# fp16 tiles transposed as 32-bit words on TensorE, for all tiles, in a matmul with rotary embedding

## The chip, the cores and the metric

One core of one Trainium2 chip runs the whole program. The metric is device time in microseconds; the kernel before took 157.14 us, the median of two runs (156.81 and 157.47).

## The reference

`x` is 16 x 512 x 768, `weight` 768 x 768, `cos` and `sin` 512 x 64, all fp32; there are 12 heads of 64. A matrix product is followed by a rotation of each head's two halves with factors that depend on the position in the sequence:

```python
y = np.matmul(x, weight).reshape(batch, seq, n_heads, head_dim)
y1, y2 = y[..., :32], y[..., 32:]
out1 = y1 * cos1 - y2 * sin1        # cos1, sin1: the first halves of cos and sin
out2 = y2 * cos2 + y1 * sin2        # cos2, sin2: the second halves
out = np.concatenate([out1, out2], axis=-1).reshape(batch, seq, hidden)
```

## The kernel before

The 8192 rows of `x` are cut into 64 tiles of 128 rows, and four tiles make a group (16 groups, numbered 0 to 15). The contraction over 768 is cut into six chunks of 128, named (t, e) with t of 3 and e of 2. Chunk (t, e) takes the columns of `x` whose index m x 6 + t x 2 + e runs over m = 0 to 127, and the rows of `weight` to match. TensorE (PE) needs each chunk of a tile with its columns on the partitions, so a tile has to be transposed before it is multiplied.

A tile goes through these steps:

- SyncE (SP) issues a DMA of the tile into one of ten buffers `xs` (`load`, L192). `pump` issues loads ahead as far as `xs` buffers are free; a buffer counts as free once its cast has been issued.
- ScalarE (ACT) casts it to fp16 into one of five buffers `xc` (`cast`, through the helper `copy`, so its line is L172). The output is contiguous in the order t, m, e; the input is read in pairs 24 bytes apart.
- PE transposes the six chunks, 128 x 128 fp16 each, into one PSUM bank `pt`, of which there are two (`turn`, L238). The data is the weight that PE loads (LDWEIGHTS), the identity `ident` is streamed.
- ACT copies the six results, 768 fp16 contiguous, into one of eight buffers `xt` (L172 as well). For tiles 0 and 1 VectorE (DVE) does this copy.
- PE multiplies: six chunks into each of two pieces of the tile's 768 output columns (512 and 256), 12 matmuls, summed in PSUM `py`, six banks (`mm_piece`, L302).
- DVE multiplies 1024 output columns at a time by cos and by sin (`rope`, L320), GpSimd (POOL) adds the two products into `ov` (L331), and `store` (L352) sends half a group at a time to memory, issued on ACT's queue. The last group goes in smaller pieces.

Twenty of the 64 tiles are not transposed on PE. `BLOCKS` names ten pairs: tiles 2 and 3 of each group from 5 to 14. A pair is loaded in four quarters (`load_quarter`, L207) laid out so that 32 x 32 blocks are what remains to be turned, and DVE turns it in one instruction, two fp16 as one 32-bit word (`turn_pair`, L263). In odd groups SP loads the pair as fp32 and ACT casts both tiles at once (`cast_pair`, L172); in even groups POOL's DMA converts to fp16 on the way and no cast is needed.

The order on every engine is written out by hand; the class `Flow` only adds semaphore waits where a buffer is read or reused. In the main loop over tiles i = 4 to 63 each iteration issues the 12 matmuls of tile i, then DVE's pair transposes (`bturns`), then PE's transposes up to tile i + `T_AHEAD` (3; tile i + 2 in the first two iterations), then the casts up to tile i + `C_AHEAD` (7), then POOL's pair loads, then the stores of the group before (after the first and third tile of a group). The prologue handles tiles 0 to 3 together with six weight chunks, which SP loads (`load_w`, L214) and DVE casts; L356 to L358 clear `cold` and build `ident`, and L413 runs twelve matmuls on zeros at the start.

Of the kernel before, what the change touches and what calls it, by code (L numbers as in the profile page):

```python
# [10 lines left out]
FP32 = mybir.dt.float32  # L11
FP16 = mybir.dt.float16
# [91 lines left out]
def kernel(  # L104
# [19 lines left out]
    R = 32  # L124
    NQ = P // R
# [9 lines left out]
    BLOCKS = {}  # L135
    for g in range(5, 15):
        BLOCKS[g, 1] = "pool" if g % 2 == 0 and g >= 4 else "sp"

    def sbuf(name, shape, dt):
        return nc.alloc_sbuf_tensor(name, shape, dt).ap()  # L140

    NX, NB, NBH, NC, NCP, NXT, NXP, NTQ, NOV = 10, 3, 3, 5, 2, 8, 4, 3, 4

    ident = sbuf("ident", [P, P], FP16)
# [6 lines left out]
    xb_b = [sbuf(f"xb{i}", [P, 2 * H], FP32) for i in range(NB)]  # L151
    xh_b = [sbuf(f"xh{i}", [P, 2 * H], FP16) for i in range(NBH)]
    xc_b = [sbuf(f"xc{i}", [P, H], FP16) for i in range(NC)]
    xd_b = [sbuf(f"xd{i}", [P, 2 * H], FP16) for i in range(NCP)]
    xt_b = [sbuf(f"xt{i}", [P, NT, 2, P], FP16) for i in range(NXT)]
    xp_b = [sbuf(f"xp{i}", [P, 2 * H], FP16) for i in range(NXP)]
# [22 lines left out]
    def pair_of(i):  # L179
        return i // QB, (i % QB) // 2  # L180

    def is_block(i):
        return pair_of(i) in BLOCKS

# [10 lines left out]

    def load_quarter(gh, q):
        g, h = gh
        b, r = where(g * QB + 2 * h)
        e = BLOCKS[gh]
        src = x[b : b + 2].rearrange("b (j a r) (q k) -> r q a (b j) k", r=SB, a=R, q=NQ)  # L200
        if q == 0:
            xs[gh] = ring("xh", NBH) if e == "pool" else ring("xb", NB)
        k = xs[gh]
        name = f"xh{k}" if e == "pool" else f"xb{k}"
        buf = xh_b[k] if e == "pool" else xb_b[k]
        dst = buf.rearrange("p (j k) -> p j k", j=2 * NQ)
        do(e, lambda eng: eng.dma_start(out=dst[ts(q, R)], in_=src[r, q]),  # L207
           writes=[f"{name}q{q}"], dma=name)
# [14 lines left out]
    def cast(i, e):  # L223
        k = xs[i]
        c = ring("xc", NC)
        xc[i] = c
        do(e, copy(e, xc_b[c].rearrange("p (t m e) -> p t m e", t=NT, e=2),
                   xs_b[k].rearrange("p (m t e) -> p t m e", t=NT, e=2)),
           reads=[f"xs{k}"], writes=[f"xc{c}"])

    def turn(i, e):
        c = xc[i]
        k = ring("pt", 2)
        z = ring("xt", NXT)
        src = xc_b[c].rearrange("p (t m e) -> p t e m", t=NT, e=2)
        pt = pt_b[k].bitcast(FP16)[:, 0:H].rearrange("p (t e m) -> p t e m", t=NT, e=2)
        for t, h in CHUNKS:
            do("pe", lambda eng: eng.transpose(pt[:, t, h, :], src[:, t, h, :], ident),  # L238
               reads=[f"xc{c}", "ident"], writes=[f"pt{k}"], tick=(t, h) == CHUNKS[-1])
        do(e, copy(e, xt_b[z], pt), reads=[f"pt{k}"], writes=[f"xt{z}"])  # L240
        xT[i] = (lambda t, h: xt_b[z][:, t, h, :], f"xt{z}")

    def cast_pair(gh, e="act"):
        k = xs[gh]
        c = ring("xd", NCP)
        xc[gh] = c
        do(e, copy(e, xd_b[c].rearrange("p (t j e) -> p t j e", t=NT, e=2),
                   xb_b[k].rearrange("p (j t e) -> p t j e", t=NT, e=2)),
           reads=[f"xb{k}q{q}" for q in range(NQ)], writes=[f"xd{c}"])

    def turn_pair(gh):
        g, h = gh
        z = ring("xp", NXP)
        dst = xp_b[z].bitcast(FP32)
        if BLOCKS[gh] == "pool":
            k = xs[gh]
            src = xh_b[k].bitcast(FP32).rearrange("p (j t) -> p t j", t=NT)
            rd = [f"xh{k}q{q}" for q in range(NQ)]
        else:
            c = xc[gh]  # L260
            src, rd = xd_b[c].bitcast(FP32), [f"xd{c}"]
        v = xp_b[z].rearrange("p (t m e) -> p t e m", t=NT, e=2)
        do("dve", lambda eng: eng.transpose(out=dst, in_=src), reads=rd, writes=[f"xp{z}"])  # L263
        for s in (0, 1):
            xT[g * QB + 2 * h + s] = (
                lambda t, e, s=s: v[:, t, e, ts(s, P)], f"xp{z}")


# [28 lines left out]
    def mm_piece(i, piece, c, start, stop, tick):  # L297
        g, s = divmod(i, QB)
        a, z, ps, bank = piece
        get, key = xT[i]  # L300
        t, h = c
        do("pe", lambda eng: eng.matmul(  # L302
            ps, get(t, h), w_sb[:, t, h, a - s * H : z - s * H], start=start, stop=stop),
            reads=[key, f"w{t}{h}"], writes=[bank], tick=tick)
# [56 lines left out]

    order = [0, 1, "w0", 2, "w1", "w2", 3, "w3", "w4", "w5"]
# [11 lines left out]
    fetch, quarters = [], []  # L374
    soon = [p for p in sorted(BLOCKS) if BLOCKS[p] == "sp"]
    for i in range(QB, NTILE):
        if soon and i >= max(2, soon[0][0] - 1) * QB:
            quarters += [(soon[0], q) for q in (0, 2, 1, 3)]
            soon.pop(0)
        if not is_block(i):  # L380
            fetch.append(i)
            if quarters:
                fetch.append(quarters.pop(0))
        elif quarters and quarters[0][0] == pair_of(i):
            fetch.append(quarters.pop(0))
    fetched = [0]
    xs_used, xb_used = [0], [0]
    xs_sent, xb_sent = [4], [0]

    def pump():  # L390

        while fetched[0] < len(fetch):
            j = fetch[fetched[0]]
            if isinstance(j, int):
                if xs_sent[0] - xs_used[0] >= NX:
                    return
                load(j)
                xs_sent[0] += 1
            else:
                if j[1] == 0:  # L400
                    if xb_sent[0] - xb_used[0] >= NB:
                        return
                    xb_sent[0] += 1
                load_quarter(*j)
            fetched[0] += 1
# [55 lines left out]
    assert not quarters  # L461
    pump()

    state = {"cast": 4, "turn": 4, "bturn": 0, "pool": 0}
    pairs = sorted(BLOCKS)
    pool_pairs = [p for p in pairs if BLOCKS[p] == "pool"]

    def casts(upto):
        while state["cast"] < min(upto, NTILE):
            i = state["cast"]  # L470
            state["cast"] += 1
            if not is_block(i):
                castx(i, "act")
            elif i % 2 == 0 and BLOCKS[pair_of(i)] == "sp":
                cast_pair(pair_of(i))
                xb_used[0] += 1
            pump()

    def turns(upto):
        while state["turn"] < min(upto, NTILE):  # L480
            i = state["turn"]
            state["turn"] += 1
            if not is_block(i):
                turn(i, "act")

    def bturns(upto):
        while state["bturn"] < len(pairs):
            gh = pairs[state["bturn"]]
            if gh[0] * QB + 2 * gh[1] >= upto:
                return  # L490
            turn_pair(gh)
            state["bturn"] += 1

    def pool_loads(upto):
        while state["pool"] < len(pool_pairs):
            gh = pool_pairs[state["pool"]]
            if gh[0] * QB + 2 * gh[1] >= upto:
                return
            for q in (0, 2, 1, 3):
                load_quarter(gh, q)  # L500
            state["pool"] += 1

    C_AHEAD, T_AHEAD, B_AHEAD, P_AHEAD = 7, 3, 6, 20
# [18 lines left out]
    for i in range(QB, NTILE):  # L522
        g, s = divmod(i, QB)
        us = units(g)
        done_to = (s + 1) * H
        for p in pieces(g, s):
            a, z, _, bank = p
            for c in CHUNKS:
                mm_piece(i, p, c, c == CHUNKS[0], c == CHUNKS[-1],
                         tick=c == CHUNKS[-1])  # L530
            for u in us:
                if u[1] == z:
                    rope(g, u)
        bturns(i + (B_AHEAD if i >= SETTLED else 3))
        turns(i + 1 + (T_AHEAD if i > QB + 1 else 2))
        casts(i + 1 + (C_AHEAD if i >= SETTLED else 3 if i == QB else 4))
        pool_loads(i + P_AHEAD)
        if s == 0 and g > 0:
            store(g - 1, 0, 2 * H, "act")
        if s == 2 and g > 0:  # L540
            store(g - 1, 2 * H, 4 * H, "act")
        if g == LAST:
            if s == 2:
                store(g, 0, H, "sp")
            if s == 3:
                store(g, H, 2 * H, "act")
# [42 lines left out]
```

## Time and profile before

| | |
|---|---|
| runs | 156.81 and 157.47 us, median 157.14 |
| profiled execution | 156.38 us, span of its instructions 154.6 us, mean granted TensorE clock 0.991 |
| PE, matmul records | 145.2 us busy, 94% of the span, 1056 instructions |
| DVE | 125.8 us, 81%, 82 instructions |
| POOL | 123.4 us, 80%, 79 instructions |
| ACT | 77.4 us, 50%, 92 instructions |
| chain that ended last | PE 84%, DVE 4%, DMA 4%, ACT 2% |
| DMA | 51.16 MB, mean 331 GB/s; 27548 packets, 7184 of them under 512 B |

A span runs from the first to the last instruction; the execution's time has 1.8 us more. Busy time is summed over a whole run whose stages differ, so a share near 100% names a suspect only. Matmuls are pipelined: a matmul's record spans from its start to its modelled end and overlaps the next one, so PE's rhythm is read from starts or from the chain, not from mean durations. L172 is the line of a helper that makes every cast and copy, and the names of the tiles tell these apart. The idle time beside a group is the wait of the engine ahead of it, with what ended it.

### The profile page before, as it was taken

The numbers are of one execution on the slowest core, as the hardware profiler recorded it, in microseconds if no ns is written. First come the engines' busy times: TensorE is split into PE (matmuls) and PEld (weight loads), VectorE is DVE, ScalarE is ACT, GpSimd is POOL, SyncE is SP. The second block draws the span as 40 slices with busy tenths as digits, with TensorE's granted clock in tenths as the row PEclk, the third lists the DMA queues.
The fourth block names the chain that finished last, engine by engine and source line by source line (L and its number), as shares of the span: only waits on it lengthen the run. The fifth ranks groups of instructions, "written<-read, shape, count | busy, mean of one in ns | idle before, by whom it ended". The sixth has DMA issues, their size and how long they took to land.

```text
span 154.6 us, 2609 instructions
## 1 busy us (share of the span) xinstructions
PE 145.2 (94%) x1056; PEld 91.9 (59%) x1056; DVE 125.8 (81%) x82; ACT 77.4 (50%) x92; POOL 123.4 (80%) x79
## 2 busy tenths in 40 slices
PE   6799999999999999999999999999999999999930
PEld 2345566666666666566666666665666666666720
DVE  0436997688777979998999899898999899997990
ACT  3462959699658615744282707452483418243000
POOL 1000599799888999799989999899988886999940
PEclk9999999999999999999999999999999999999996
DMA  4999999999999999999999999999999963443983
GB/s 138 387 408 397 403 399 401 368 342 362 372 344 302 395 350 336 358 381 363 351 332 385 391 347 318 365 405 368 368 368 360 382 251 139 155 179 150 374 336 106
DMA packets 27548, 51.16 MB, mean 331 GB/s; under 512 B 7184, under 2 KB 13072, under 8 KB 27536
## 3 DMA queue, kind: packets, MB, share of 16 engines
q1 hardware_dynamic: 13504, 24.78, 45.7%
q10 hardware_dynamic: 8592, 24.25, 39.9%
q0 software_dynamic: 5440, 1.97, 10.3%
q8 instruction: 8, 0.13, 0.3%
q14 instruction: 4, 0.03, 0.1%
HBM read 27.79 MB, written 25.17 MB: 343 GB/s over the span
## 4 chain that ended last, share of the span: by engine, by line
PE 84%; DVE 4%; DMA 4%; ACT 2%; SPq 1%; issue 1%; DVEq 0%
PE py L302 76%; PE pt L238 9%; DMA w_raw<-in_weight_dram 4%; DVE xs L320 1%; ACT xc L172 1%; DVE tq L320 1%; DVE ov L331 1%; SPq L192 1%; DVE w_raw L320 1%; SPq L214 1%; ACT xt L172 1%; DVE w_sb L172 0%; DVEq L55 0%; SPq L584 0%; SPq L114 0%
## 5 line engine op out<-in xcount | busy, mean ns | idle before, releaser
L302 PE MATMUL py<-w_sb,xt 128*128 128x256 f16 (+1 forms) x528 | 89.9, 323 | 1.4 <-DVE w_sb L172 1.1
L331 POOL TENSOR_TENSOR ov<-tq 128x1024 f32<-128x1024 f32 (+2 forms) x33 | 68.9, 2105 | 21.6 <-DVE tq L320 21.4
L320 DVE TENSOR_TENSOR tq<-py,csn 128x2048 f32<-128x2048 f32 (+2 forms) x33 | 66.4, 2024 | 9.3 <-PE py L302 8.9
L302 PEld LDWEIGHTS py<-w_sb,xt 128*128 128x128 f16 x528 | 50.3, 98 | 32.6 <-DVE w_sb L172 2.8
L172 ACT COPY xt<-pt 128x768 f16<-128x768 f16 x42 | 33.5, 800 | 56.1 <-PE pt L238 56.1
L320 DVE TENSOR_TENSOR w_raw<-py,csn 128x2048 f32<-128x2048 f32 (+1 forms) x20 | 41.4, 2068 | 5.8 <-PE py L302 5.7
L331 POOL TENSOR_TENSOR ov<-w_raw 128x1024 f32<-128x1024 f32 (+1 forms) x20 | 42.8, 2149 | 2.6 <-DVE w_raw L320 2.6
L172 ACT CAST xc<-xs 128x768 f16<-128x768 f32 x44 | 39.2, 905 | 8.6 <-DMA xs<-in_x_dram 8.4
L302 PE MATMUL py<-w_sb,xp 128*128 128x512 f16 (+1 forms) x240 | 42.3, 326 | 0.0
L302 PEld LDWEIGHTS py<-w_sb,xp 128*128 128x128 f16 x240 | 22.6, 98 | 12.9
L238 PE MATMUL pt<-ident,xc 128*128 128x128 f16 x264 | 21.9, 219 | 0.2 <-ACT xc L172 0.2
L238 PEld LDWEIGHTS pt<-ident,xc 128*128 128x128 f16 x264 | 18.0, 98 | 6.8 <-ACT xc L172 2.0
L207 POOL DMA_DIRECT2D xh<-in_x_dram x20 | 11.7, 590 | 0.0
L172 ACT CAST xd<-xb 128x1536 f16<-128x1536 f32 x5 | 8.0, 1603 | 0.0
L263 DVE STREAM_TRANSPOSE xp<-xh 128x768 f32<-128x768 f32 x5 | 6.2, 1246 | 0.0
L172 DVE CAST w_sb<-w_raw 128x768 f16<-128x768 f32 x6 | 3.4, 559 | 3.5 <-DMA w_raw<-in_weight_dram 3.5
L413 PE MATMUL py<-cold 128*128 128x512 f16 x12 | 4.6, 552 | 1.4 <-DVE cold L356 1.4
L172 DVE COPY xt<-pt 128x768 f16<-128x768 f16 x2 | 1.1, 558 | 4.8 <-PE pt L238 4.8
L263 DVE STREAM_TRANSPOSE xp<-xd 128x768 f32<-128x768 f32 x5 | 4.8, 968 | 0.0
L413 PEld LDWEIGHTS py<-cold 128*128 128x128 f16 x12 | 1.4, 131 | 3.4 <-issue 1.9
L172 ACT ACT_TABLE_LOAD x1 | 1.3, 1283 | 0.9 <-SPq L114 0.9
L302 PE MATMUL pt<-w_sb,xt 128*128 128x256 f16 x12 | 1.5, 272 | 0.0
(13 smaller groups left out, 6.8 us busy)
## 6 DMA issues: line engine op xcount, KB each, us to landing
out_dram<-ov ACTq DMA_DIRECT2D x30, 768.0 KB, 8.3
xs<-in_x_dram SPq DMA_DIRECT2D x44, 384.0 KB, 16.2
xb<-in_x_dram SPq DMA_DIRECT2D x20, 192.0 KB, 16.5
w_raw<-in_weight_dram SPq DMA_DIRECT2D x6, 384.0 KB, 6.7
xh<-in_x_dram POOLq DMA_DIRECT2D x20, 96.0 KB, 12.3
out_dram<-ov SPq DMA_DIRECT2D x1, 384.0 KB, 2.8
out_dram<-ov ACTq DMA_DIRECT2D x1, 384.0 KB, 2.5
out_dram<-ov SPq DMA_DIRECT2D x1, 256.0 KB, 2.0
```

The lines of the kernel that those rows point to most:

```text
L172: eng.copy(out=o, in_=i_) if e == "act" else eng.tensor_copy(out=o, in_=i_)
L192: do(e, lambda eng: eng.dma_start(out=xs_b[k], in_=x[b].rearrange("(p r) h -> r p h", r=SB)[r]), writes=[f"xs{k}"], dma=f"xs{k}")
L207: do(e, lambda eng: eng.dma_start(out=dst[ts(q, R)], in_=src[r, q]), writes=[f"{name}q{q}"], dma=name)
L214: do(e, lambda eng: eng.dma_start(out=w_raw[:, t, h], in_=wv[t, h]), writes=[f"wr{t}{h}"], dma=f"w{t}{h}")
L238: do("pe", lambda eng: eng.transpose(pt[:, t, h, :], src[:, t, h, :], ident), reads=[f"xc{c}", "ident"], writes=[f"pt{k}"], tick=(t, h) == ...
L263: do("dve", lambda eng: eng.transpose(out=dst, in_=src), reads=rd, writes=[f"xp{z}"])
L302: do("pe", lambda eng: eng.matmul(ps, get(t, h), w_sb[:, t, h, a - s * H : z - s * H], start=start, stop=stop), reads=[key, f"w{t}{h}"], w ...
L320: do("dve", lambda eng: eng.tensor_tensor(out=tq.rearrange("p j (h d) -> p j h d", d=D), in0=ps.rearrange("p (h d) -> p h d", d=D) .unsque ...
L331: do(adder, lambda eng: eng.tensor_tensor(out=ov_b[o][:, ds(c0, w)].rearrange("p (h t d) -> p h t d", t=2, d=HD), in0=tq[:, 0].rearrange(" ...
L413: do("pe", lambda eng: eng.matmul(py[:, ts(b, 512)], cold[:, 0:P], cold, start=True, stop=warmed[0] < WARM - 6), reads=["cold"], writes=[f ...
```

## The change

All 64 tiles now take the same way, and the pairs with their loads, casts, buffers and DVE transposes are gone. `xc` has room for a 32-bit word per value. The cast writes each fp16 into the lower half of its word, in the order t, e, m; the upper halves are zeroed once, by POOL, ahead of the first load. PE transposes the words as fp32 with an fp32 identity. Six chunks of 128 words no longer fit into one bank of 512 words, so a tile takes both `pt` banks, three chunks in each, and each half has its own copy into `xt`, which reads every second fp16. The matmuls wait for the half that holds their chunk. `xs` has 14 buffers (10 before), `xc` 6 (5 before), and casts are issued 5 tiles ahead (7 before).

```diff
-    BLOCKS = {}
-    for g in range(5, 15):
-        BLOCKS[g, 1] = "pool" if g % 2 == 0 and g >= 4 else "sp"
...
-    NX, NB, NBH, NC, NCP, NXT, NXP, NTQ, NOV = 10, 3, 3, 5, 2, 8, 4, 3, 4
-    ident = sbuf("ident", [P, P], FP16)
+    NX, NC, NXT, NTQ, NOV = 14, 6, 8, 4, 4
+    ident = sbuf("ident", [P, P], FP32)
...
-    xc_b = [sbuf(f"xc{i}", [P, H], FP16) for i in range(NC)]
-    xt_b = [sbuf(f"xt{i}", [P, NT, 2, P], FP16) for i in range(NXT)]
+    xc_b = [sbuf(f"xc{i}", [P, 2 * H], FP16) for i in range(NC)]
+    xt_b = [sbuf(f"xt{i}", [P, H], FP16) for i in range(NXT)]
...
     def cast(i, e):
-        do(e, copy(e, xc_b[c].rearrange("p (t m e) -> p t m e", t=NT, e=2),
+        do(e, copy(e, xc_b[c].rearrange("p (t e m z) -> p t e m z", t=NT, e=2, z=2)[:, :, :, :, 0]
+                   .rearrange("p t e m -> p t m e"),
                    xs_b[k].rearrange("p (m t e) -> p t m e", t=NT, e=2)),
...
     def turn(i, e):
         c = xc[i]
-        k = ring("pt", 2)
         z = ring("xt", NXT)
-        src = xc_b[c].rearrange("p (t m e) -> p t e m", t=NT, e=2)
-        pt = pt_b[k].bitcast(FP16)[:, 0:H].rearrange("p (t e m) -> p t e m", t=NT, e=2)
-        for t, h in CHUNKS:
-            do("pe", lambda eng: eng.transpose(pt[:, t, h, :], src[:, t, h, :], ident),
-               reads=[f"xc{c}", "ident"], writes=[f"pt{k}"], tick=(t, h) == CHUNKS[-1])
-        do(e, copy(e, xt_b[z], pt), reads=[f"pt{k}"], writes=[f"xt{z}"])
-        xT[i] = (lambda t, h: xt_b[z][:, t, h, :], f"xt{z}")
+        src = xc_b[c].bitcast(FP32)
+        for half in (0, 1):
+            k = ring("pt", 2)
+            pt = pt_b[k][:, 0 : H // 2]
+            for t in range(NT):
+                do("pe", lambda eng: eng.transpose(
+                    pt[:, ts(t, P)], src[:, ts(NT * half + t, P)], ident),
+                   reads=[f"xc{c}", "ident"], writes=[f"pt{k}"], tick=t == NT - 1)
+            do(e, copy(e, xt_b[z][:, ts(half, H // 2)],
+                       pt.bitcast(FP16).rearrange("p (n z) -> p n z", z=2)[:, :, 0]),
+               reads=[f"pt{k}"], writes=[f"xt{z}h{half}"])
+        xT[i] = (lambda t, h: xt_b[z][:, ts(2 * t + h, P)], f"xt{z}")
...
-            reads=[key, f"w{t}{h}"], writes=[bank], tick=tick)
+            reads=[f"{key}h{(2 * t + h) // 3}", f"w{t}{h}"], writes=[bank], tick=tick)
...
+    for c in range(NC):
+        do("pool", lambda eng: eng.memset(xc_b[c], 0.0), writes=[f"xc{c}"])
...
-    C_AHEAD, T_AHEAD, B_AHEAD, P_AHEAD = 7, 3, 6, 20
+    C_AHEAD, T_AHEAD = 5, 3
...
-        bturns(i + (B_AHEAD if i >= SETTLED else 3))
         turns(i + 1 + (T_AHEAD if i > QB + 1 else 2))
         casts(i + 1 + (C_AHEAD if i >= SETTLED else 3 if i == QB else 4))
-        pool_loads(i + P_AHEAD)
```

With `BLOCKS` go `load_quarter`, `cast_pair`, `turn_pair`, `bturns`, `pool_loads` and the list of quarters in `pump`, which now issues whole tiles in order.

More of the change, by code (lines that the diff above doesn't have):

```diff
@@ L123 @@
     HD = D // 2
-    R = 32
-    NQ = P // R
     NT = H // (2 * P)
@@ L150 @@
     xs_b = [sbuf(f"xs{i}", [P, H], FP32) for i in range(NX)]
-    xb_b = [sbuf(f"xb{i}", [P, 2 * H], FP32) for i in range(NB)]
-    xh_b = [sbuf(f"xh{i}", [P, 2 * H], FP16) for i in range(NBH)]
-    xc_b = [sbuf(f"xc{i}", [P, H], FP16) for i in range(NC)]
-    xd_b = [sbuf(f"xd{i}", [P, 2 * H], FP16) for i in range(NCP)]
-    xt_b = [sbuf(f"xt{i}", [P, NT, 2, P], FP16) for i in range(NXT)]
-    xp_b = [sbuf(f"xp{i}", [P, 2 * H], FP16) for i in range(NXP)]
+    xc_b = [sbuf(f"xc{i}", [P, 2 * H], FP16) for i in range(NC)]
+    xt_b = [sbuf(f"xt{i}", [P, H], FP16) for i in range(NXT)]
     tq_b = [sbuf(f"tq{i}", [P, 2, 1024], FP32) for i in range(NTQ)]
@@ L177, in where @@
         return QB * (g // SB) + s, g % SB
[L179 to L183, printed above, removed]
     xs, xc, xT = {}, {}, {}
@@ L194, in load @@
             writes=[f"xs{k}"], dma=f"xs{k}")
[L196 to L208, printed above, removed]
     wv = weight.rearrange("(p t e) n -> t e p n", t=NT, e=2)
@@ L232, in turn @@
         c = xc[i]
-        k = ring("pt", 2)
         z = ring("xt", NXT)
-        src = xc_b[c].rearrange("p (t m e) -> p t e m", t=NT, e=2)
-        pt = pt_b[k].bitcast(FP16)[:, 0:H].rearrange("p (t e m) -> p t e m", t=NT, e=2)
-        for t, h in CHUNKS:
-            do("pe", lambda eng: eng.transpose(pt[:, t, h, :], src[:, t, h, :], ident),
-               reads=[f"xc{c}", "ident"], writes=[f"pt{k}"], tick=(t, h) == CHUNKS[-1])
-        do(e, copy(e, xt_b[z], pt), reads=[f"pt{k}"], writes=[f"xt{z}"])
-        xT[i] = (lambda t, h: xt_b[z][:, t, h, :], f"xt{z}")
[L243 to L266, printed above, removed]
+        src = xc_b[c].bitcast(FP32)
[10 more added lines that the diff above has]
+        xT[i] = (lambda t, h: xt_b[z][:, ts(2 * t + h, P)], f"xt{z}")
     def units(g):
@@ L371 @@
         out=sin_sb, in_=sin.rearrange("(p r) d -> p r d", r=SB)), writes=["sin"], dma="sin")
[L374 to L388, printed above, removed]
-    def pump():
[L392 to L405, printed above, removed]
+    sent, xs_used = [4], [0]
+    def pump():
+        while sent[0] < NTILE and sent[0] - xs_used[0] < NX:
+            load(sent[0])
+            sent[0] += 1
     WARM = 12
@@ L460 @@
         reads=["sin", "csn1", "cos"], writes=["csn"])
-    assert not quarters
     pump()
-    state = {"cast": 4, "turn": 4, "bturn": 0, "pool": 0}
-    pairs = sorted(BLOCKS)
-    pool_pairs = [p for p in pairs if BLOCKS[p] == "pool"]
+    state = {"cast": 4, "turn": 4}
     def casts(upto):
         while state["cast"] < min(upto, NTILE):
-            i = state["cast"]
+            castx(state["cast"], "act")
             state["cast"] += 1
[L472 to L476, printed above, removed]
             pump()
@@ L480, in turns @@
         while state["turn"] < min(upto, NTILE):
-            i = state["turn"]
+            turn(state["turn"], "act")
             state["turn"] += 1
[L483 to L501, printed above, removed]
-    C_AHEAD, T_AHEAD, B_AHEAD, P_AHEAD = 7, 3, 6, 20
+    C_AHEAD, T_AHEAD = 5, 3
     SETTLED = 2 * QB
```

## The prediction

> **What bounds the kernel now.** I read the page's busy table first, then the chain of work that ended last in order of time, then the stretches, then the groups by form, and last the timelines of PE and ACT.
>
> ```profile
> PE 145.2 (94%) x1056; PEld 91.9 (59%) x1056; DVE 125.8 (81%) x82; ACT 77.4 (50%) x92; POOL 123.4 (80%) x79
> ```
>
> PE is nearly always busy and, by the page, carries 84% of the chain (DMA 4%). DVE and POOL at 80% look close behind, so the share alone decides nothing. The chain in order of time does:
>
> ```profile
> 43.52 0.33 PE pt L238 x6
> 43.86 1.95 PE py L302 x12
> ```
>
> ```profile
> 53.00 5.85 PE py L302 x36
> 59.18 1.95 PE py L302 x12
> 61.47 5.85 PE py L302 x36
> ```
>
> Before 53 us every tile is 12 matmuls (1.95 us) and 6 transposes (0.33 to 0.34 us): one tile each (50.71 - 27.86) / 10 = 2.285 us. From group 5 on, a group of four tiles has 48 matmuls but only two sets of transposes: 61.47 - 53.00 = 8.47 us, which is 4 x 1.95 + 2 x 0.335. So even there the rhythm is the sum of PE's own instructions and nobody makes it wait. The stretches say the same:
>
> ```profile
> 27.86:48.43 20.57, 20.57 (x165) 13.64 (x163) 15.75 (x7) 16.78 (x21) 17.70 (x12) 1.00 1.10 353
> 53.00:137.70 84.70, 84.70 (x602) 53.68 (x601) 77.93 (x42) 38.88 (x45) 78.99 (x44) 1.00 1.00 334
> ```
>
> The columns are the length, then PE, PEld, DVE, ACT and POOL busy, the granted clock, the DMA share, GB/s. PE fills both stretches at the full clock. In the second, ACT is at 46%, DVE at 92%, POOL at 93%. Each microsecond added to PE from 25 to 142 us is therefore a microsecond of the result, until another engine takes longer per tile than PE.
>
> **The rows that price the parts.**
>
> ```profile
> L172 ACT CAST xc<-xs 128x768 f16<-128x768 f32 x44 | 39.2, 905 | 8.6 <-DMA xs<-in_x_dram 8.4
> ...
> L172 ACT COPY xt<-pt 128x768 f16<-128x768 f16 x42 | 33.5, 800 | 56.1 <-PE pt L238 56.1
> ...
> L238 PE MATMUL pt<-ident,xc 128*128 128x128 f16 x264 | 21.9, 219 | 0.2 <-ACT xc L172 0.2
> L238 PEld LDWEIGHTS pt<-ident,xc 128*128 128x128 f16 x264 | 18.0, 98 | 6.8 <-ACT xc L172 2.0 <-issue 0.7
> ...
> L172 ACT CAST xd<-xb 128x1536 f16<-128x1536 f32 x5 | 8.0, 1603 | 0.0
> ...
> L263 DVE STREAM_TRANSPOSE xp<-xh 128x768 f32<-128x768 f32 x5 | 6.2, 1246 | 0.0
> ...
> L263 DVE STREAM_TRANSPOSE xp<-xd 128x768 f32<-128x768 f32 x5 | 4.8, 968 | 0.0
> ...
> L172 DVE COPY xt<-pt 128x768 f16<-128x768 f16 x2 | 1.1, 558 | 4.8 <-PE pt L238 4.8
> ```
>
> A transpose's record of 219 ns is latency; in the chain six of them take 0.335 us, 56 ns each. Its weight load of 98 ns is hidden entirely under the matmul before it.
>
> **The change part by part.** The sum is made against the profiled execution: 156.38 us, of which 154.6 is the span. It lies 0.76 us under the median of the runs, 157.14.
>
> *More tiles go through TensorE.* Ten block pairs, 20 tiles, had no TensorE transposes. Now they have: 20 x 0.335 = 6.7 us, all on the path, since PE fills the stretch where they land. This is the sure part.
>
> *The price of one transpose with 4-byte elements.* All 384 (64 x 6) are now of 32-bit words; the 264 of before were 16-bit. The trace has no 32-bit transpose. Lower bound: the 12 matmuls of a tile stream 4608 columns in 1.95 us, 0.423 ns each, so 128 columns need 54 ns; today's 56 ns is already that, and no row shows PE faster, so I exclude a gain. Upper bounds: 98 ns if the weight load, record as now, sets the pace; 154 ns if load and matmul run one after the other; 216 ns (4 x 54) if the word takes four passes. I take 56 ns: the changed program still issues one weight load and one 128-column matmul for each transpose, so the row nearest to it is the present transpose. The other ends are rivals below: 384 x 42 ns = 16.1 us, 384 x 98 = 37.6 us, 384 x 160 = 61.4 us.
>
> [...]
>
> *Two evictions per tile in place of one.* Each half is 384 elements, read from PSUM at every second fp16. From the two casts: (1603 - 905) / 768 = 0.91 ns per element and 207 ns fixed; the 800 ns copy then has 0.77 ns per element, and a half costs 207 + 384 x 0.77 = 0.50 us. Bounds: 0.40 (half of 800) and 0.80 (no saving). ACT overlaps neighbours by 0.1 us:
>
> ```profile
> 30.18 0.80 ACT L172 COPY xt<-pt 128x768 f16<-128x768 f16 x1 [0.68 <-PE pt L238]
> 30.20 0.38 ACTq L352 DMA_DIRECT2D out_dram<-ov  x1
> 30.88 3.30 ACT L172 CAST xc<-xs 128x768 f16<-128x768 f32 x4
> ```
>
> From start to start a copy takes 0.70 us (30.18 to 30.88), a cast 0.80 ((3.30 - 0.905) / 3), and the store's issue on ACT's queue (30.20) delays nothing. So ACT's new tile is 2 x 0.40 + 0.80 = 1.60 us against PE's 2.285: hidden, with 0.68 us left. At the upper bound, 2 x 0.70 + 0.80 = 2.20, it still just hides. What waits behind: PE's next set needs both banks empty, but that is a tile later.
>
> *The cast now scatters* each fp16 into a word of its own, neighbours in the input landing 512 bytes apart. No row has such a write on ACT; the nearest is DVE's pair 968 / 1246 ns, the same transpose from two source layouts, x1.29. Bounds: unchanged 0.905 us, and twice that. I take 0.905; x1.29 (1.17 us) hides as well. ACT is late only from a cast of about 0.80 + 0.68 + 0.10 = 1.6 us.
>
> *Back-to-back sets.* At one tile of group 1 two sets of transposes follow each other (12 in a row in the instruction order). A set now takes both banks, so the second waits for two copies: 0.22 us of matmul latency + 0.50 + about 0.1 of semaphores - 0.17 for the other trio = 0.6 us, and 0.2 for the second bank: 0.8 us on PE. Bounds 0 and 1.7 (a cast ahead of the copies).
>
> *Start.* DVE evicts tiles 0 and 1 in two halves of 0.36 (its 0.52 ns per element) to 0.57 us (twice that) in place of 0.56; the second ends 0.2 to 0.8 us later, and the cast of the first weight chunk is queued behind it. The chain takes its third weight chunk at 9.48 us from DMA, so most of this hides; I count 0.3 us, bounds 0 and 0.8. Six clears of xc go to POOL ahead of the first cast: POOL's 128-element clear takes 0.20 us and a one-element one 0.10, so 1536 elements cost 0.7 (as words) to 1.4 us. The first is done by 2.8 us, the cast that needs it starts at 4.20 after its DMA; the sixth by 9.8, needed after 15. Nothing, or 1 us if a clear is twice as slow.
>
> *What goes.* DVE loses ten transposes (11.0 us), POOL 20 DMA issues (11.7 us), SP trades 20 quarter loads for 20 whole tiles. None gains: PE waited for none of them. SP's queue has 14 tiles of lead, 14 x 2.285 = 32 us against 16.2 us to landing; SP is moved past nothing. The cast's lead shrinks from 7 tiles to 5, still 11 us.
>
> Sum: 6.7 + 0 + 0.8 + 0.3 = 7.8 us. 156.38 + 7.8 = 164.2; with the 0.76 us to the median, **165 us**.
>
> **Rivals.**
> - *Weight load paces the transposes.* Place: PE, each set. For it: the load carries twice the bytes per element, and at 98 ns its record already exceeds 56. Against: it hides completely today. 165 + 16.1 = 181 us; in series with its matmul, 165 + 37.6 = 203.
> - *Four passes.* 165 + 61.4 = 226 us. Against: the instruction count is unchanged.
> - *ACT becomes the bound through the scattered cast.* From 1.6 us on; at twice the present (1.81 us, 1.70 from start to start) a tile takes 2.50 us: 60 tiles x 0.215 = 13 us, 178 us; with evictions of 0.80 us as well 2 x 0.70 + 1.70 = 3.10, which is beyond my range (214 us).
> - *Not slower: DMA, not PE, sets the end.* The DMA row is at 9 tenths nearly throughout, and the 7184 packets under 512 B and the POOL queue's 10.3% go away. Then a PE that works 6.7 us more has room, and the time stays at 156 to 158 us; it decides only if PE idles 6.7 us in 53 to 138 us today. Against: PE is busy 84.70 of 84.70 us there, and DMA is 4% of the chain, at the start.
>
> **How the numbers follow.** My forecast, 163 to 168 us: 0.55. Weight load in the way: 0.24, of which 0.18 at or under 192 us. ACT bound: 0.09, mostly 172 to 190. Four passes: 0.09. Not slower: 0.03. From 162 (the sum with its small terms at zero is 163.8, less scatter) to 192 us leaves out 0.06 + 0.09 + 0.03 = 0.18. A 2% change is about what a measurement of this kernel tells from none: faster 0.01, within 2% 0.04 (the DMA case, or all small terms negative), slower 0.95.
>
> **What would show it.** Right: the chain keeps 1.95 us for 12 matmuls with 0.33 to 0.34 us of transposes between *every* two tiles to the end, 64 sets; ACT's half copies near 0.50 us, casts near 0.9; PE waits for ACT only around the 12 in a row. Wrong: sets of 0.6 us or more (load) or 1.3 (passes); a cast of 1.6 us with PE idle on ACT; or PE idle that today is absent.

## The result and the profile after

The changed kernel takes 294.0 us (293.91 and 294.08) against 157.14 us: a ratio of 1.873, interval 1.868 to 1.879. The forecast was 165 us, 162 to 192. Its direction was right, its size far off: the time grew by 136.9 us, not 7.8. The profiled execution took 293.91 us, its span 292.1 us.

The page of the changed kernel, busy table and two rows of the 40 slices:

```profile
PE 196.6 (67%) x1176; PEld 119.7 (41%) x1176; DVE 117.7 (40%) x74; ACT 270.5 (93%) x189; POOL 120.6 (41%) x65
...
PE   5579574776776676667666766776677667666781
...
ACT  4979989999999999999999999999999999999930
```

PE has fallen from 94% to 67%, and ACT has risen from 50% to 93%; it is busy from the first tile to the last cast. The chain has moved with it:

```profile
ACT 75%; issue 16%; PE 4%; DVE 2%; DMA 1%; ACTq 0%; SPq 0%; DVEq 0%
ACT xc L162 54%; ACT xt L162 20%; PE pt L210 3%; DMA xs<-in_x_dram 1%; DVE xs L268 1%; PE py L250 1%; DVE tq L268 1%; DVE ov L279 0%; ACT L162 0%; DVE w_raw L268 0%; DVE xt L162 0%; DVE w_sb L162 0%; ACTq L300 0%; DVEq L55 0%; SPq L480 0%
```

More than half of the chain is one kind of instruction, the cast into `xc`. The groups by form of the changed kernel (busy us, mean ns, idle before and releaser) give its price:

```profile
L162 ACT CAST xc<-xs 128x768 f16<-128x768 f32 x64 | 243.8, 3849 | 0.0
...
L162 ACT COPY xt<-pt 128x384 f16<-128x384 f16 x124 | 84.1, 831 | 5.5 <-PE pt L210 5.5
...
L210 PE MATMUL pt<-ident,xc 128*128 128x128 f32 x384 | 61.0, 297 | 86.6 <-ACT xt L162 74.1 <-ACT xc L162 12.5
...
L210 PEld LDWEIGHTS pt<-ident,xc 128*128 128x128 f32 x384 | 42.0, 145 | 115.8 <-ACT xt L162 94.6 <-ACT xc L162 15.9 <-issue 1.9
```

The cast of the same 768 values per partition went from 905 to 3849 ns, 4.25 times. PE waits 86.6 us for ACT ahead of its transposes, where it had waited 0.2. The copy's mean of 831 ns is not its price: ACT's records overlap, and a copy queued behind a slow cast is recorded from before that cast's end. The smallest copy took 477 ns. The timeline of ACT shows the beat:

```profile
102.07 3.75 ACT L162 CAST xc<-xs 128x768 f16<-128x768 f32 x1
102.95 0.38 ACTq L300 DMA_DIRECT2D out_dram<-ov  x1
105.20 1.32 ACT L162 COPY xt<-pt 128x384 f16<-128x384 f16 x2
106.27 3.77 ACT L162 CAST xc<-xs 128x768 f16<-128x768 f32 x1
```

From cast to cast it is 106.27 - 102.07 = 4.20 us per tile, against 2.285 us of PE before. In the chain, that is about 3.52 us of cast and 0.69 us for two copies. The "issue" of the chain (16%) lies inside such casts: its piece from 103.33 to 105.20 us falls into the cast recorded from 102.07 to 105.82. 64 tiles of 4.20 us are 269 us of the 292.1.

### The profile page after: what moved, and what is told of

Read it like the earlier page. It is cut to its first block, busy times and chain, and to the rows that moved or that the text cites. A ratio compares the mean times of both kernels' runs of the same rounds, so it can differ in the third digit from the quotient of the medians.

```text
span 292.1 us, 2900 instructions
## 1 busy us (share of the span) xinstructions
PE 196.6 (67%) x1176; PEld 119.7 (41%) x1176; DVE 117.7 (40%) x74; ACT 270.5 (93%) x189; POOL 120.6 (41%) x65
## 4 chain that ended last, share of the span: by engine, by line
ACT 75%; issue 16%; PE 4%; DVE 2%; DMA 1%; ACTq 0%; SPq 0%; DVEq 0%
ACT xc L162 54%; ACT xt L162 20%; PE pt L210 3%; DMA xs<-in_x_dram 1%; DVE xs L268 1%; PE py L250 1%; DVE tq L268 1%; DVE ov L279 0%; ACT L162 0%; DVE w_raw L268 0%; DVE xt L162 0%; DVE w_sb L162 0%; ACTq L300 0%; DVEq L55 0%; SPq L480 0%
## 5 line engine op out<-in xcount | busy, mean ns | idle before, releaser
L162 ACT CAST xc<-xs 128x768 f16<-128x768 f32 x64 | 243.8, 3849 | 0.0
L250 PE MATMUL py<-w_sb,xt 128*128 128x256 f16 (+1 forms) x768 | 139.4, 333 | 1.1 <-DVE w_sb L162 1.1
L279 POOL TENSOR_TENSOR ov<-tq 128x1024 f32<-128x1024 f32 (+2 forms) x36 | 75.7, 2107 | 119.8 <-DVE tq L268 119.6
L210 PE MATMUL pt<-ident,xc 128*128 128x128 f32 x384 | 61.0, 297 | 86.6 <-ACT xt L162 74.1
L250 PEld LDWEIGHTS py<-w_sb,xt 128*128 128x128 f16 x768 | 76.7, 100 | 46.1 <-issue 4.7
L210 PEld LDWEIGHTS pt<-ident,xc 128*128 128x128 f32 x384 | 42.0, 145 | 115.8 <-ACT xt L162 94.6
L162 ACT COPY xt<-pt 128x384 f16<-128x384 f16 x124 | 84.1, 831 | 5.5 <-PE pt L210 5.5
L279 POOL TENSOR_TENSOR ov<-w_raw 128x1024 f32<-128x1024 f32 (+2 forms) x17 | 36.4, 2138 | 44.6 <-DVE w_raw L268 44.5
L268 DVE TENSOR_TENSOR w_raw<-py,csn 128x2048 f32<-128x2048 f32 (+2 forms) x17 | 35.2, 2072 | 46.5 <-PE py L250 46.3
L311 POOL MEMSET xc<- 128x1536 f16 x6 | 8.0, 1378 | 0.0
```

The costliest lines, as they stand in the source:

```text
L162: eng.copy(out=o, in_=i_) if e == "act" else eng.tensor_copy(out=o, in_=i_)
L210: do("pe", lambda eng: eng.transpose(pt[:, ts(t, P)], src[:, ts(NT * half + t, P)], ident), reads=[f"xc{c}", "ident"], writes=[f"pt{k}"], ...
L250: do("pe", lambda eng: eng.matmul(ps, get(t, h), w_sb[:, t, h, a - s * H : z - s * H], start=start, stop=stop), reads=[f"{key}h{(2 * t + h ...
L268: do("dve", lambda eng: eng.tensor_tensor(out=tq.rearrange("p j (h d) -> p j h d", d=D), in0=ps.rearrange("p (h d) -> p h d", d=D) .unsque ...
L279: do(adder, lambda eng: eng.tensor_tensor(out=ov_b[o][:, ds(c0, w)].rearrange("p (h t d) -> p h t d", t=2, d=HD), in0=tq[:, 0].rearrange(" ...
L311: do("pool", lambda eng: eng.memset(xc_b[c], 0.0), writes=[f"xc{c}"])
```

## The experiments

Two readings stood at the outset. **Theory A**: a 2-byte write that leaves half of its 4-byte word alone is slow on ACT. **Theory B**: successive writes to places far apart are slow. Both explain the cast. Whether the 32-bit transposes alone would have cost anything was open too, since PE was never the bound in this profile. Each experiment is the changed kernel with one edit, unless it says otherwise; the diffs show the lines that matter, and the line numbers of the kernels differ a little. Where no ratio is given, the kernel ran once.

**The pairs alone.** `ident`, `xc`, `xt` and `turn` are as in the kernel before (six 16-bit transposes, one bank, one copy), and the clears are gone:

```diff
-        do(e, copy(e, xc_b[c].rearrange("p (t e m z) -> p t e m z", t=NT, e=2, z=2)[:, :, :, :, 0]
-                   .rearrange("p t e m -> p t m e"),
+        do(e, copy(e, xc_b[c].rearrange("p (t m e) -> p t m e", t=NT, e=2),
```

> The pairs alone are removed: all 64 tiles go through 16-bit transposes on PE, the cast writes its fp16 next to each other in the order it reads them, one copy per tile as before. Theory A (a 2-byte write that does not fill a 4-byte word together with its neighbour is slow on ACT) and theory B (successive writes to places far apart are slow) both expect a cast of 0.9 us and PE as the bound: 156.4 + 20 x 0.335 = 163 us, ratio 1.04. If instead the loss of the pairs is itself costly (ACT or DMA), it is above 168 us.

Measured: 163.44 us, ratio 1.041 (1.037 to 1.045). Cast 901 ns, and PE the bound with one set after every tile. The chain of this kernel:

```profile
62.13 0.34 PE pt L208 x6
62.46 1.95 PE py L245 x12
64.41 0.34 PE pt L208 x6
64.75 1.95 PE py L245 x12
```

So giving up the ten pairs costs 6.3 us. The 130 us above that come from how the words are written, transposed and copied out.

**Scattered, but no half-empty words.** As the kernel of the pairs alone, with `xc` in another order:

```diff
-        do(e, copy(e, xc_b[c].rearrange("p (t m e) -> p t m e", t=NT, e=2),
+        do(e, copy(e, xc_b[c].rearrange("p (t e m) -> p t m e", t=NT, e=2),
...
-        src = xc_b[c].rearrange("p (t m e) -> p t e m", t=NT, e=2)
+        src = xc_b[c].rearrange("p (t e m) -> p t e m", t=NT, e=2)
```

> As e1, but the cast writes its fp16 in the order t, e, m, so successive values land 256 bytes apart and neighbours in memory are written at different times; no word is left half empty. Theory A: the writes never come in pairs, so the cast takes 3.5 to 3.9 us and the time is near 290 us. Theory B: also slow, 290 us. If only the empty upper halves matter, the cast takes 0.9 us and the time is 163 us.

Measured: 286.2 us, cast 3651 ns:

```profile
L162 ACT CAST xc<-xs 128x768 f16<-128x768 f32 x64 | 231.2, 3651 | 2.2 <-DMA xs<-in_x_dram 2.2
```

No word is left half empty here, all transposes are 16-bit, and nearly the whole loss is back. The empty halves are not needed for it.

**Scattered, whole words.** ACT copies fp32 to fp32 into the same scattered order, and the copy out of PSUM rounds to fp16; no upper halves need clearing, so the clears are gone:

```diff
-    xc_b = [sbuf(f"xc{i}", [P, 2 * H], FP16) for i in range(NC)]
+    xc_b = [sbuf(f"xc{i}", [P, H], FP32) for i in range(NC)]
...
+        do(e, copy(e, xc_b[c].rearrange("p (t e m) -> p t m e", t=NT, e=2),
```

> The changed kernel with whole words: ACT copies fp32 to fp32 in the same scattered order (512 bytes apart), PE transposes the fp32 words, the copy out of PSUM rounds to fp16. Theory A: whole words are written, the cast takes 0.9 us, and PE is the bound with sets of six 32-bit transposes at 0.65 us: 154.6 + 6.7 + 64 x 0.315 + 1.8 = 183 us. Theory B: the cast takes 3.5 to 3.9 us, 290 us.

Measured: 186.7 us, ratio 1.191 (1.184 to 1.197), the copy into `xc` 1592 ns:

```profile
L162 ACT COPY xc<-xs 128x768 f32<-128x768 f32 x64 | 101.0, 1592 | 3.2 <-DMA xs<-in_x_dram 3.2
```

This is between the two theories: 4-byte writes in the same places are slowed, but far less than 2-byte ones. With ACT out of the way, PE is the bound, and its chain shows what a 32-bit transpose costs:

```profile
62.43 0.65 PE pt L209 x6
63.08 1.95 PE py L249 x12
65.03 0.66 PE pt L209 x6
65.69 1.95 PE py L249 x12
```

A set of six takes 0.655 us where the 16-bit set took 0.335: 109 ns each in place of 56.

**Half words in order.**

```diff
-        do(e, copy(e, xc_b[c].rearrange("p (t e m z) -> p t e m z", t=NT, e=2, z=2)[:, :, :, :, 0]
-                   .rearrange("p t e m -> p t m e"),
+        do(e, copy(e, xc_b[c].rearrange("p (t m e z) -> p t m e z", t=NT, e=2, z=2)[:, :, :, :, 0],
...
-        src = xc_b[c].bitcast(FP32)
+        src = xc_b[c].bitcast(FP32).rearrange("p (t m e) -> p t e m", t=NT, e=2)
```

> The changed kernel with the words in the order in which they are read (t, m, e): each write still fills half a word, but successive writes are 4 bytes apart; PE reads every second word. Theory A: cast 3.5 to 3.9 us, 290 us. Theory B: cast 0.9 to 1.0 us, PE the bound, 183 us.

Measured: 189.7 us, cast 1077 ns. Theory A falls: writes that each fill half a word, 4 bytes apart, cost 0.18 us more than neighbouring fp16 (901 ns). PE now loads every second word as its weights. Its groups in this kernel:

```profile
L209 PE MATMUL pt<-ident,xc 128*128 128x128 f32 x384 | 57.0, 285 | 2.3 <-ACT xc L162 2.1 <-ACT xt L162 0.2
...
L209 PEld LDWEIGHTS pt<-ident,xc 128*128 128x128 f32 x384 | 53.9, 206 | 7.8 <-ACT xc L162 2.6 <-ACT xt L162 0.4 <-DVE xt L162 0.3
```

Against the kernel with whole words, the weight load's record grew by 65 ns (141 to 206), the set only to 0.70 to 0.72 us, some 9 ns a transpose. A load that ran in series with its matmul would have added all 65, as far as a record's length is the load's time.

**Output order.** Same places as the changed kernel, visited in the order of the output:

```diff
-                   .rearrange("p t e m -> p t m e"),
-                   xs_b[k].rearrange("p (m t e) -> p t m e", t=NT, e=2)),
+                   xs_b[k].rearrange("p (m t e) -> p t e m", t=NT, e=2)),
```

> The changed kernel, same places for every value, but the cast goes through them in the order of the output (m innermost): writes 4 bytes apart, reads 24 bytes apart one by one. Theory C (it is the write side: ACT pays about 4.6 ns for a 2-byte write that lands far from the one before it): cast near the 1.08 us of in-order half words, PE the bound, 187 to 190 us. Rival (the price sits in going through memory in jumps on either side): the cast stays above 2 us and ACT the bound, over 200 us.

Measured: 189.75 us, PE the bound, as theory C had it, but the cast took 1625 ns and not 1.08 us:

```profile
L162 ACT CAST xc<-xs 128x768 f16<-128x768 f32 x64 | 103.5, 1625 | 0.0
```

Visiting the output in order removes most of the price, which is therefore on the write side. Single reads 24 bytes apart cost 0.55 us over the pairwise reads of the half words in order. This one edit takes 104 us off the changed kernel.

**How far is far.** 16-bit transposes as in the kernel of the pairs alone; successive writes alternate between two places whose distance depends on the buffer (6, 18, 66 and 258 bytes, `xca` to `xcd`, two buffers of each). From one value to the next the cast steps forward by that distance and then back by 4 bytes less:

```diff
+    FAR, W = [3, 9, 33, 129], 384
...
+    def xc_at(c, ap):
+        return bass.AP(xc_b[c].tensor, 0, [[NT * W, P], [W, NT]] + ap)
...
+        do(e, copy(e, xc_at(c, [[2, P], [FAR[c % 4], 2]]),
```

> 16-bit transposes for all tiles (as e1, 163 us), with xc laid out so that successive writes of the cast alternate between two places whose distance differs by buffer: 6, 18, 66 and 258 bytes for the buffers a, b, c, d; PE always reads every second fp16. Theory C with a short line in which successive writes are gathered: a threshold, near 0.9 us below it and near 3.6 us above it; which of the four are slow gives its size. Rival (any step other than to the next address is slow): all four near 3.6 us. With two of four slow, ACT takes 2 x 1.5 + 2 x 4.2 = 11.4 us a group against PE's 9.1, some 200 us.

Measured: 239.3 us; the time only mixes the four casts, which are the point. Groups by form of this kernel:

```profile
L163 ACT CAST xcc<-xs 128x768 f16<-128x768 f32 x16 | 59.7, 3729 | 0.0
L163 ACT CAST xcd<-xs 128x768 f16<-128x768 f32 x16 | 58.7, 3668 | 0.0
...
L163 ACT CAST xcb<-xs 128x768 f16<-128x768 f32 x16 | 53.4, 3340 | 0.1
...
L163 ACT CAST xca<-xs 128x768 f16<-128x768 f32 x16 | 15.0, 940 | 2.4 <-DMA xs<-in_x_dram 2.4
```

Three are slow, not two: my guess of 200 us fell with that. At 6 bytes the cast is nearly as fast as in order (901 ns), at 18 it is slow, from 66 on distance no longer matters. The threshold of this pattern lies between 6 bytes (940 ns) and 18 (3340 ns). The 6-byte case alone doesn't tell a short distance from a word that gets filled, since its steps back of 2 bytes complete the word just begun; the half words in order, 4 bytes apart with no word filled, do (1077 ns). From 66 bytes on the price over 0.90 us is 2.80 us (3.70 as the mean of the two), at 18 bytes it is 2.44 us, an eighth less; why is not shown.

**Whole words in order.** As the kernel with whole words, in reading order:

```diff
-        do(e, copy(e, xc_b[c].rearrange("p (t e m) -> p t m e", t=NT, e=2),
+        do(e, copy(e, xc_b[c].rearrange("p (t m e) -> p t m e", t=NT, e=2),
...
-        src = xc_b[c]
+        src = xc_b[c].rearrange("p (t m e) -> p t e m", t=NT, e=2)
```

> As e3 (whole fp32 words), but written in the order in which they are read; PE reads every second word. This is the price of a 4-byte copy without jumps: near 0.9 us if the 1.59 us of e3 was due to the scatter, near 1.6 us if 4-byte output is that slow by itself. PE is the bound either way: 187 to 190 us.

Measured: 188.2 us, the copy 912 ns. So 1592 ns is the scatter: 0.68 us for 768 four-byte writes, against 2.75 us for as many two-byte ones.

**Two neighbours, then a jump.** As the kernel of the pairs alone, same places; the order of writing changes:

```diff
-        do(e, copy(e, xc_b[c].rearrange("p (t m e) -> p t m e", t=NT, e=2),
-                   xs_b[k].rearrange("p (m t e) -> p t m e", t=NT, e=2)),
+        do(e, copy(e, xc_b[c].rearrange("p (t m e) -> p m t e", t=NT, e=2),
+                   xs_b[k].rearrange("p (m t e) -> p m t e", t=NT, e=2)),
```

> As e1 (16-bit transposes for all tiles, xc in the order t, m, e, cast 0.90 us, 163 us), but the cast goes m, t, e: it reads in the order of memory and writes two neighbouring fp16, then jumps 512 bytes. [...] If each such write costs by itself, the cast takes 0.90 + (3.65 - 0.90) / 2 = 2.3 us, ACT needs 2.2 + 0.7 = 2.9 us a tile, some 200 us. If two hits in a row are enough to absorb the price, or the two are merged into one 4-byte write, it takes 0.9 to 1.6 us (384 jumps at e3's 0.9 ns more each), PE stays the bound, 163 us.

Measured: 163.4 us, cast 885 ns, no slower than in order:

```profile
L162 ACT CAST xc<-xs 128x768 f16<-128x768 f32 x64 | 56.4, 885 | 6.1 <-DMA xs<-in_x_dram 5.9
```

A jump of 512 bytes after every second write costs nothing that shows, far from the 2.3 us of a price for each of the 384 writes after a jump; the same edit lets the cast read without jumps, so that a small price could be offset. What is dear is a 2-byte write whose neighbours in time both lie elsewhere (3340 ns a cast at 18 bytes, 3651 at 256). Why one near neighbour is enough is not shown. If two neighbours cost as much as one 4-byte write, 384 of them at the 2.07 ns of the whole scattered words (1592 / 768) take 0.8 us, which would be hidden as well: an estimate that agrees with the 885 ns, from one run.

**Another engine.** Every second cast of the main loop goes to DVE:

```diff
-            castx(state["cast"], "act")
+            castx(state["cast"], "dve" if state["cast"] % 2 else "act")
```

> The changed kernel with the casts of every second tile from tile 4 on given to DVE, same places, same order. If the scattered write is slow on ACT alone, DVE's casts take 0.6 to 1.6 us, ACT needs 3.5 + 4 x 0.35 = 4.9 us for two tiles, PE 2 x 2.6 = 5.2, and the time is 187 to 195 us. If the memory is slow for any engine, DVE's casts take 3 us or more too, DVE needs 3.4 + 3.6 = 7 us for two tiles, and the time is near 245 us.

Measured: 226.7 us, DVE's casts 2806 ns, ACT's 3686:

```profile
L162 DVE CAST xc<-xs 128x768 f16<-128x768 f32 x30 | 83.8, 2806 | 0.0
```

Neither forecast met, but nearer the second: the price is not ACT's alone. DVE casts 768 values in order in 0.55 us (its weight casts), so it takes five times as long. The fastest of its 30 casts still took 2.53 us. POOL's additions rose from 2.37 to 2.93 and 3.27 us meanwhile; whether POOL beside it adds to DVE's price is not shown. ACT's casts do not explain that price alone: the cast on DVE that began at 104.86 us took 2.57 us though ACT's next cast began only at 106.86 us.

**What paces a 32-bit transpose.** Two edits on top of the whole scattered words. The first streams half as many columns under the same loads, the second loads half as many under the same streams:

```diff
+                for u in (0, 1):
+                    do("pe", lambda eng: eng.transpose(
+                        pt[:, ts(2 * t + u, P // 2)], src[0 : P // 2, ts(NT * half + t, P)],
+                        ident[0 : P // 2, 0 : P // 2]),
```

> On top of whole scattered words (ratio 1.19, sets of six at 0.655 us): each 32-bit transpose becomes two, each loading 128 columns of weights from the tile's first 64 rows and streaming 64 columns of the identity; the second 64 rows of each tile are replaced by its first. If the stream of a 32-bit transpose runs at two cycles a column, 12 x 54.5 = 0.655 us a set, 187 us. If the 32-bit weight load sets the pace at 109 ns, 12 x 109 = 1.31 us a set, 187 + 64 x 0.655 = 229 us. If load and stream take 54 ns each one after the other, 12 x 82 = 0.98 us, 208 us.

```diff
+                for u in (0, 1):
+                    do("pe", lambda eng: eng.transpose(
+                        pt[0 : P // 2, ts(t, P)], src[:, ts(2 * (NT * half + t) + u, P // 2)],
+                        ident),
```

> The counterpart of e6, which came out between the theories: as e3 (sets of six at 0.655 us), but each 32-bit transpose becomes two, each loading 64 columns of weights and streaming the whole identity of 128 columns; both write partitions 0 to 63, and partitions 64 to 127 of the bank hold zeros from a clear at the start, so half of each tile's contraction is left out. If the stream sets the pace at two cycles a column, 109 ns each, 12 x 109 = 1.31 us a set, 187 + 64 x 0.655 = 229 us. If load and stream of 54 ns each follow one another, 12 x (27 + 54) = 0.98 us, 208 us. If the load sets the pace at 109 ns for 128 columns, 12 x 56 = 0.67 us, 187 us.

The chain of the kernel with short streams:

```profile
102.40 0.90 PE pt L210 x12
103.30 2.06 PE py L251 x12
105.35 0.89 PE pt L210 x12
```

The weight loads of the first of these sets with short streams, on PE's timeline:

```profile
102.33 0.83 PEld L210 LDWEIGHTS pt<-ident,xc 64*128 64x128 f32 x12 [0.21 <-issue]
```

The chain of the kernel with short loads:

```profile
103.97 1.31 PE pt L210 x12
105.28 1.95 PE py L251 x12
107.23 1.31 PE pt L210 x12
```

Short streams: 206.0 us, 0.89 to 0.90 us a set, 75 ns each, none of the three forecasts (0.655, 0.98, 1.31 us a set) clearly. More than half of the gap to 0.655 lies at the two ends of a set: within it the twelve loads take 0.83 us and the last of them 0.14, so one comes every 63 ns, and the transposes follow each other as closely (six in 0.37 us of the chain). A load paced at 109 ns is excluded, since here 128 columns are loaded every 63 ns (of 64 rows; the record, 139 ns, is that of a load of 128 rows, 141). Short loads: 226.95 us and 1.31 us a set, the forecast of a stream that takes 109 ns for 128 columns, twice the time of a 16-bit one: half the load saves nothing. The records agree. A 32-bit transpose of 128 columns is recorded with 273 ns, as is a 16-bit matmul of 256 columns; a 16-bit transpose with 219. Why short streams follow each other at 63 ns and not at 54 stays open.

**Two values per word.** The cast writes fp16 in reading order, and PE sees two of them as one word; one bank, one copy of 768 fp16:

```diff
+        src = xc_b[c].bitcast(FP32)
+        pt = pt_b[k][:, 0 : H // 2]
+        for t in range(NT):
+            do("pe", lambda eng: eng.transpose(pt[:, ts(t, P)], src[:, ts(t, P)], ident),
```

> 32-bit transposes with a value in both halves of the word: the cast writes fp16 in reading order (0.9 us), PE transposes three times 128 words per tile, one copy brings 768 fp16 to SBUF, the matmuls read every second fp16. With 109 ns for a 32-bit transpose a set takes 0.327 us against the 0.335 of six 16-bit ones: 163 us, ratio 1.04, the same as e1. If a set has a fixed cost of its own, or the weight load of the first transposes shows, it is slower: 168 us or more.

Measured: 163.36 us, ratio 1.039 (1.036 to 1.041); a set of three takes 0.33 us. A word with both halves used makes up for the double price exactly, and gains nothing over 16-bit transposes.

## Why the prediction was wrong

- *What bounds the kernel, and the pairs (6.7 us)*: right. The kernel without pairs is 6.3 us slower, with PE's rhythm as read.
- *"The cast now scatters ... Bounds: unchanged 0.905 us, and twice that. I take 0.905"*: this is the step that failed. It measured 3.85 us, 4.25 times, so the bounds failed and not only the choice. No row of the trace had such a write, and the nearest that I took was a read on another engine (x1.29). The threshold of that step, a cast of 1.6 us, was not tested: with 32-bit transposes PE takes 1.95 + 0.655 = 2.605 us a tile and not 2.285, and at 1625 ns (output order) PE was still the bound. The mechanism of the rival "ACT becomes the bound through the scattered cast" is what happened; with the measured 3.52 us and 0.69 us per tile its sum gives 165 + 60 x (4.21 - 2.285) = 280 us, and I had given it 0.09 and priced it at 178 to 214. Half of the 14 us that are still missing are lost at the start: the first matmuls with weights begin at 15.41 us instead of 7.82.
- *"I take 56 ns"* for a transpose: wrong too, 109 ns. Whole scattered words show the cost without ACT in the way: 64 x 0.32 = 20.5 us of the 23.3 us between 163.4 and 186.7. The other 2.8 us are lost in the first dozen tiles: from 22.4 to 38.8 us the chain of that kernel still runs over ACT's casts and copies, and only then over PE alone. The rival that came nearest to this time (181 us) named the weight load; short loads and strided loads show that it is the stream. My argument, one load and one matmul as before, says how many instructions there are and not how long each is. Four passes for a word had no row behind them either, and no run shows them: 109 against 56 ns is twice.
- *Two evictions*: right, 0.48 us unobstructed against 0.50 foreseen, 0.345 from start to start.
- *Back-to-back sets and the other engines*: without weight once ACT is the bound. With the whole words in order, where ACT is not in the way, the two sets took 1.94 us instead of 2 x 0.71, some 0.5 us more against the 0.8 foreseen. The 0.1 us for semaphores in that term had no row behind it; the chain of the changed kernel shows 0.02 to 0.04 us between two engines (at 59.51 and 60.12 us). *Start*: DVE's halves took 0.56 us each, the upper end of 0.36 to 0.57. The six clears took 8.0 us on POOL and hid, as foreseen, but something that came with them did not: ACT's first cast now waits for two engines, DMA and POOL, and ACT's table load starts only behind the wait for DMA, at 4.32 us instead of 0.91, so that the first cast starts at 5.62 us instead of 4.20. The other three kernels with the clears show it too (4.3 to 4.6 us); those without have the load at 0.9.
- *Not slower*: no. DMA is at 1% of the chain.

The differences between the runs, which add up by themselves: 157.1 + 6.3 (pairs) + 23.3 (32-bit transposes) + 107.3 (2-byte casts scattered in place of whole words, ACT the bound) = 294.0 us.

## What to carry to other kernels

Before a layout is changed for one engine, follow the order in which the engine ahead writes it: for each value, which values come before and after in time, and whether one of them lies close by (here 4 and 6 bytes were close enough, at 1077 and 940 ns a cast, and 18 were not, at 3340). If none does and the write is 2 bytes, count on four times the price, as here (3849 against 905 ns), and let the loop run over the output's order (1625), or write two neighbours at a time (885). An operation that the trace has never shown in the new width is not priced by the old row: let the range reach at least to the ratio of the widths, which was the price here (109 against 56 ns).

## What the runs showed that I had not expected

- ACT, 768 values per partition, fp32 in: 0.90 us written in order as fp16; 0.94 alternating over 6 bytes; 1.08 in steps of 4 bytes; 3.34 alternating over 18 bytes; 3.65 to 3.85 from 66 to 512 bytes; 0.885 as neighbouring twos 512 bytes apart. As fp32: 0.91 in order, 1.59 scattered over 512 bytes.
- DVE pays for the same scatter, 2.81 us against 0.55 in order (the latter for its weight casts).
- Clears that had time to spare still moved ACT's table load from 0.9 us to between 4.3 and 4.6 us.
- A transpose of 128 columns on PE: 56 ns in 16 bits, 109 ns in 32 bits, 118 ns if the 32-bit weights are read at every second word.
